# Fetching gamma's row as seven small transfers instead of one, in an RMSNorm and SiLU kernel on one core

## The chip, the cores and the metric

The kernel runs on one core of a Trainium2 chip. The metric is the device time of one execution in microseconds (us), median of three runs. In this document a "load" brings a block of `x` from HBM into on-chip memory and a "store" takes a finished block back. TensorE, VectorE and ScalarE appear in the profile as PE, DVE and ACT; SP and ACT issue the transfers, and their issuing queues appear as SPq and ACTq. The 16 DMA engines of the core move the bytes for both queues. In the tables of DMA queues q10 carries what ACT issues and q1 what SP issues.

## The reference

```python
def reference(x, gamma, eps):          # x: 8 x 1024 x 2048, gamma: 2048, all float32
    rms = np.sqrt(np.mean(x ** 2, axis=-1, keepdims=True) + eps)
    out = gamma * x / rms
    return (out * (1 / (1 + np.exp(-out)))).astype(np.float32)
```

Each of the 8192 rows of 2048 numbers is divided by its root mean square, multiplied by gamma, and put through SiLU. The input is 67.1 MB and so is the output.

## The kernel before

The rows are cut into 16 blocks of 512 rows. A block is one tile `xt` of 128 partitions; each partition holds 4 rows (`J = 4`), so that a load or a store of a block is one transfer of 4 MB in which every partition has one contiguous piece of 32 KB. Six such tiles exist (`BUFS = 6`). The work is done in place: a block is loaded (line 54, issued on ACT's queue), its sums of squares are taken (two or one of its rows by ScalarE, line 65, the others by VectorE, line 73), the root is taken on ScalarE (line 82) and inverted on VectorE (line 87), VectorE multiplies each row by its reciprocal root and by gamma (line 92), ScalarE applies SiLU to the block in two halves (line 98), and SP issues the store (line 102). The last block goes a little differently (lines 153 to 160): it is multiplied by gamma first, and its SiLU takes the reciprocal root as a scale (line 158).

The order of each engine's work is written out by hand. What matters for the change is the head, lines 106 to 119, in the order of the program:

- load 0 is issued on ACT's queue (line 106); VectorE fills the tile `ones` (line 107); ScalarE runs one tiny activation (line 109).
- SP fetches gamma's row, 8 KB, into partition 0 of the tile `g` (line 110), and then issues a small store of `ones` to 16 pieces of 512 bytes in the output's first block (line 111), which store 0 later overwrites.
- TensorE spreads gamma over the 128 partitions: four chunks of 512 columns, each a multiplication of a column of ones with the chunk of the row in partition 0, into `junk_v` in PSUM (line 114). A float32 chunk shows as two matmuls in the profile.
- load 1 is issued on ACT's queue (line 115).
- VectorE copies the whole of `junk_v` back over `g` (line 116), and ScalarE copies one element of `junk_v` (line 117). ScalarE's copy waits for VectorE's.
- Only behind that copy, on ACT's queue, come loads 2 to 5 (lines 118 and 119).

Then the squares of block 0 begin. Inside the main loop, load `b + 3` is issued on ACT's queue after the first row of squares of block `b + 1` (lines 65 to 69). For the first three blocks (`SOON = 3`) the multiplication of block `b` comes ahead of the squares of block `b + 1`; later it comes behind them.

The framework gives each transfer one of eight completion semaphores in turn, in the order of the program, and the queue that issues a transfer first waits until the transfer that had the same semaphore before has landed. In program order the transfers before the change are load 0, gamma, the store of `ones`, loads 1 to 5 (the first eight), then store 0, store 1, store 2, load 6 and so on, 34 in all.

Of the kernel before, what the change touches and what calls it, by code (L numbers as in the profile page):

```python
# [1 line left out]

# [4 lines left out]

ACT = mybir.ActivationFunctionType
ALU = mybir.AluOpType


@with_exitstack
def kernel(
    ctx: ExitStack,
    tc: tile.TileContext,
    x: bass.AP,
    gamma: bass.AP,
    eps: bass.AP,
    out: bass.AP,
):  # L20

    nc = tc.nc
    P = nc.NUM_PARTITIONS
    f32 = mybir.dt.float32
    x2 = x.flatten_outer_dims()
    o2 = out.flatten_outer_dims()  # L30
    n, d = x2.shape
    J = 4
    BUFS = 6
    nblk = n // (P * J)
    xb = x2.rearrange("(b p j) d -> b p (j d)", p=P, j=J)
    ob = o2.rearrange("(b p j) d -> b p (j d)", p=P, j=J)

    singles = ctx.enter_context(tc.tile_pool(name="singles", bufs=1))
    pool = ctx.enter_context(tc.tile_pool(name="pool", bufs=BUFS))
    small = ctx.enter_context(tc.tile_pool(name="small", bufs=2))  # L40
    psum = ctx.enter_context(tc.tile_pool(name="psum", bufs=1, space=bass.MemoryType.PSUM))

    Q = 4
    w = d // Q
    g = singles.tile([P, d], f32)
    eps_t = singles.tile([P, 1], f32)
    ones = singles.tile([P, P], f32)
    junk_a = psum.tile([P, d], f32, name="junk_a")
    junk_v = psum.tile([P, d], f32, name="junk_v")
    blocks, sss, rmss, rstds = {}, {}, {}, {}  # L50

    def load(b):
        xt = pool.tile([P, J * d], f32, name="xt")
        nc.scalar.dma_start(out=xt, in_=xb[b])  # L54
        blocks[b] = xt

    def row(b, j):
        return blocks[b][:, j * d:(j + 1) * d]

    def squares_scalar(b, loads=()):  # L60


        sss[b] = small.tile([P, J], f32, name="ss")
        for j in range(share(b)):
            nc.scalar.activation(out=junk_a, in_=row(b, j), func=ACT.Square,  # L65
                                 accum_out=sss[b][:, j:j + 1])
            if j == 0:
                for s in loads:
                    load(s)

    def squares_vector(b):
        for j in range(share(b), J):
            nc.vector.tensor_tensor_reduce(  # L73
                out=junk_v, in0=row(b, j), in1=row(b, j), scale=1.0, scalar=0.0,
                op0=ALU.mult, op1=ALU.add, accum_out=sss[b][:, j:j + 1])

    def share(b):
        return 1 if 4 <= b <= 12 and b % 2 == 0 else 2

    def root(b):  # L80
        rms = small.tile([P, J], f32, name="rms")
        nc.scalar.activation(out=rms, in_=sss.pop(b), func=ACT.Sqrt, scale=1.0 / d, bias=eps_t)  # L82
        rmss[b] = rms

    def invert(b):
        rstd = small.tile([P, J], f32, name="rstd")
        nc.vector.reciprocal(out=rstd, in_=rmss.pop(b))  # L87
        rstds[b] = rstd

    def multiply(b):  # L90
        for j in range(J):
            nc.vector.scalar_tensor_tensor(out=row(b, j), in0=row(b, j), scalar=rstds[b][:, j:j + 1],  # L92
                                           in1=g, op0=ALU.mult, op1=ALU.mult)

    def silu(b):
        for h in range(0, J, 2):
            cols = slice(h * d, (h + 2) * d)
            nc.scalar.activation(out=blocks[b][:, cols], in_=blocks[b][:, cols], func=ACT.Silu)  # L98
        store(b)

    def store(b):
        nc.sync.dma_start(out=ob[b], in_=blocks[b])

    with tc.manual_schedule():

        load(0)
        nc.vector.memset(ones, 1.0)  # L107
        nc.vector.memset(eps_t, float(eps))
        nc.scalar.activation(out=junk_a[:, 0:1], in_=ones[:, 0:1], func=ACT.Square)  # L109
        nc.sync.dma_start(out=g[0:1, :], in_=bass.AP(tensor=gamma.tensor, offset=gamma.offset, ap=[[d, 1], [1, d]]))  # L110
        nc.sync.dma_start(out=ob[0][::P // 16, 0:P], in_=ones[::P // 16, :])
        for c in range(Q):
            cols = slice(c * w, (c + 1) * w)
            nc.tensor.matmul(junk_v[:, cols], ones[0:1, :], g[0:1, cols], start=True, stop=True)  # L114
        load(1)
        nc.vector.tensor_copy(out=g, in_=junk_v)  # L116
        nc.scalar.copy(out=junk_a[:, 0:1], in_=junk_v[:, d - 1:d])  # L117
        for b in range(2, BUFS):
            load(b)

        last = nblk - 1
        SOON = 3
        squares_scalar(0)
        squares_vector(0)
        root(0)
        invert(0)
        for b in range(last):
            loads = [b + 3] if BUFS <= b + 3 < nblk else []  # L130
            if b < SOON:
                multiply(b)
                squares_scalar(b + 1, loads)
                silu(b)
                squares_vector(b + 1)
                root(b + 1)
            elif b < last - 1:
                squares_scalar(b + 1, loads)
                squares_vector(b + 1)
                root(b + 1)  # L140
                multiply(b)
                silu(b)
            else:
                multiply(b)
                squares_scalar(b + 1)
                silu(b)
                squares_vector(b + 1)
                root(b + 1)
            if b + 1 < last:
                invert(b + 1)  # L150


        for j in range(J):
            if j == J // 2:
                invert(last)
            nc.vector.tensor_mul(out=row(last, j), in0=row(last, j), in1=g)  # L156
        for j in range(J):
            nc.scalar.activation(out=row(last, j), in_=row(last, j), func=ACT.Silu,  # L158
                                 scale=rstds[last][:, j:j + 1])
        store(last)  # L160


# [1 line left out]
_INS = ['x', 'gamma', 'eps']  # L164
_OUTS = [((8, 1024, 2048), 'float32')]

_NUMBERS = {'eps': 9.999999747378752e-06}


# [26 lines left out]
```

## Time and profile before

| what | value |
|---|---|
| median of 3 runs | 316.97 us (316.83 to 317.03) |
| the profiled execution's own time | 316.86 us |
| its span, first to last instruction | 315.1 us |
| VectorE busy | 235.4 us, 75% of the span |
| ScalarE busy | 213.9 us, 68% |
| TensorE matmuls | 7.2 us, 2%, eight matmuls |
| transfers of 4 MB | 16 loads on ACT's queue, 16 stores on SP's queue |
| bytes moved | 134.25 MB, mean 426 GB/s over the span |

The span is shorter than the execution's time by 1.8 us, which lie outside the first and last instruction. The page of the profile cuts the span into 40 equal slices and gives, for each, the busy share of each engine in tenths, the mean busy share of the 16 DMA engines and the rate. Its chain of work is followed back from the last instruction and tells what released what. The waits give, for each engine and line, how long the engine stood and what ended that. A packet, in the tables of DMA queues, is one contiguous piece moved by one DMA engine, or the small write of 4 bytes with which that engine reports that its part of a transfer is done.

### The profile page before, as it was taken

What the parts mean: (1) busy time and instruction counts of PE and PEld (TensorE: products, weight loads), DVE (VectorE), ACT (ScalarE), POOL (GpSimd) and SP (SyncE); (2) the same over time, 40 slices, a digit from 0 to 9 for tenths busy, and PEclk for the clock granted to TensorE, in tenths of its full rate; (3) what the DMA queues carried; (4) which work ended last, traced back from release to release, by engine and by line L of the source; (5) the groups of instructions that cost most, each with busy time, mean ns of one, the idle gap of its engine ahead of it and who ended that gap; (6) DMA issues with size and microseconds to landing.
All of it is one profiled execution on the core that took longest, in us unless ns stands there. A gap on an engine that the chain in (4) does not pass through costs nothing.

```text
span 315.1 us, 440 instructions
## 1 busy us (share of the span) xinstructions
PE 7.2 (2%) x8; PEld 2.5 (1%) x8; DVE 235.4 (75%) x157; ACT 213.9 (68%) x137; POOL 0.2 (0%) x4
## 2 busy tenths in 40 slices
PE   6200000000000000000000000000000000000000
PEld 2000000000000000000000000000000000000000
DVE  0679697979995795957959489593995939999600
ACT  1169998972799268782687727876278768779910
POOL 0000000000000000000000000000000000000000
DMA  8999999999999999999999999999999999999996
GB/s 331 408 458 412 395 458 404 458 412 453 416 454 416 446 416 449 416 449 416 449 420 449 416 449 420 449 416 449 424 441 428 437 433 433 433 433 433 433 433 300
DMA packets 4644, 134.25 MB, mean 426 GB/s; under 512 B 529, under 2 KB 545, under 8 KB 545
## 3 DMA queue, kind: packets, MB, share of 16 engines
q10 hardware_dynamic: 2304, 67.11, 49.7%
q1 hardware_dynamic: 2338, 67.13, 49.4%
q14 instruction: 2, 0.02, 0.0%
HBM read 67.12 MB, written 67.12 MB: 426 GB/s over the span
## 4 chain that ended last, share of the span: by engine, by line
DMA 68%; DVE 14%; ACT 11%; issue 1%; ACTq 1%; DVEq 0%
DMA xt<-in_x_dram 68%; DVE xt L92 9%; DVE junk_v L73 5%; ACT xt L98 4%; ACT junk_a L65 3%; ACT xt L158 2%; ACT L82 1%; ACTq L191 1%; ACT L158 0%; ACT L98 0%; ACT rms L82 0%; DVE ss L73 0%; DVE rstd L87 0%; ACTq L54 0%; ACT L109 0%
## 5 line engine op out<-in xcount | busy, mean ns | idle before, releaser
L92 DVE SCALAR_TENSOR_TENSOR xt<-xt,rstd,g 128x2048 f32<-128x2048 f32 x60 | 137.0, 2346 | 0.1
L98 ACT ACTIVATE xt<-xt 128x4096 f32<-128x4096 f32 x30 | 108.3, 3615 | 27.1 <-DVE xt L92 27.1
L73 DVE CUSTOM_DVE_ANT_0 junk_v<-xt 128x2048 f32<-128x2048 f32 x37 | 85.1, 2299 | 42.4 <-DMA xt<-in_x_dram 41.7
L65 ACT ACTIVATE junk_a<-xt 128x2048 f32<-128x2048 f32 x27 | 50.6, 1876 | 16.1 <-DMA xt<-in_x_dram 14.0
L82 ACT ACT_TABLE_LOAD x15 | 19.2, 1283 | 26.6 <-DVE ss L73 26.5
L98 ACT ACT_TABLE_LOAD x14 | 18.0, 1283 | 0.2
L116 DVE COPY g<-junk_v 128x2048 f32<-128x2048 f32 x1 | 2.3, 2292 | 9.1 <-PE junk_v L114 9.1
L87 DVE RECIPROCAL rstd<-rms 128x4 f32<-128x4 f32 x16 | 2.8, 173 | 8.4 <-ACT rms L82 8.4
L156 DVE TENSOR_TENSOR xt<-xt,g 128x2048 f32<-128x2048 f32 x4 | 9.0, 2280 | 0.0
L82 ACT ACTIVATE rms<-ss,eps_t 128x4 f32<-128x4 f32 x16 | 4.8, 297 | 5.7 <-DVE ss L73 5.5
L158 ACT ACTIVATE xt<-xt,rstd 128x2048 f32<-128x2048 f32 x4 | 7.7, 1991 | 0.0
L114 PE MATMUL junk_v<-g,ones 1*128 1x512 f32 x8 | 7.2, 1072 | 2.9 <-DMA g<-in_gamma_dram 2.9
L117 ACT COPY junk_a<-junk_v 128x1 f32<-128x1 f32 x1 | 0.1, 144 | 9.9 <-DVE g L116 9.9
L73 DVE DVE_READ_ACCUMULATOR2_ANT ss<- 128x1 f32 x37 | 5.2, 140 | 0.0
L65 ACT ACTIVATION_READ_ACCUMULATOR junk_a<-xt 128x1 f32 x27 | 5.0, 186 | 0.0
L114 PEld LDWEIGHTS junk_v<-g,ones 1*128 1x128 f32 x8 | 2.5, 327 | 6.0 <-issue 6.0
L109 ACT ACT_TABLE_LOAD x1 | 1.3, 1283 | 1.1 <-PEq L177 1.1
L158 ACT ACT_TABLE_LOAD x1 | 1.3, 1283 | 0.0
L107 DVE MEMSET ones<- 128x128 f32 x1 | 0.2, 165 | 0.8 <-PEq L177 0.8
L109 ACT ACTIVATE junk_a<-ones 128x1 f32<-128x1 f32 x1 | 0.2, 174 | 0.0
L177 POOL MEMSET const-bfloat16-1.0<- 128x1 bf16 x1 | 0.1, 102 | 0.0
L177 POOL MEMSET const-uint8-127<- 128x1 uint8 x1 | 0.1, 102 | 0.0
(3 smaller groups left out, 0.3 us busy)
## 6 DMA issues: line engine op xcount, KB each, us to landing
xt<-in_x_dram ACTq DMA_DIRECT2D x16, 4096.0 KB, 38.7
out_dram<-xt SPq DMA_DIRECT2D x16, 4096.0 KB, 32.1
g<-in_gamma_dram SPq DMA_DIRECT2D x1, 8.0 KB
out_dram<-ones SPq DMA_DIRECT2D x1, 8.0 KB, 7.1
```

Source lines behind the costliest of these rows:

```text
L65: nc.scalar.activation(out=junk_a, in_=row(b, j), func=ACT.Square, accum_out=sss[b][:, j:j + 1])
L73: nc.vector.tensor_tensor_reduce(out=junk_v, in0=row(b, j), in1=row(b, j), scale=1.0, scalar=0.0, op0=ALU.mult, op1=ALU.add, accum_out=sss ...
L82: nc.scalar.activation(out=rms, in_=sss.pop(b), func=ACT.Sqrt, scale=1.0 / d, bias=eps_t)
L87: nc.vector.reciprocal(out=rstd, in_=rmss.pop(b))
L92: nc.vector.scalar_tensor_tensor(out=row(b, j), in0=row(b, j), scalar=rstds[b][:, j:j + 1], in1=g, op0=ALU.mult, op1=ALU.mult)
L98: nc.scalar.activation(out=blocks[b][:, cols], in_=blocks[b][:, cols], func=ACT.Silu)
L109: nc.scalar.activation(out=junk_a[:, 0:1], in_=ones[:, 0:1], func=ACT.Square)
L114: nc.tensor.matmul(junk_v[:, cols], ones[0:1, :], g[0:1, cols], start=True, stop=True)
L116: nc.vector.tensor_copy(out=g, in_=junk_v)
L156: nc.vector.tensor_mul(out=row(last, j), in0=row(last, j), in1=g)
L158: nc.scalar.activation(out=row(last, j), in_=row(last, j), func=ACT.Silu, scale=rstds[last][:, j:j + 1])
L191: with _tile.TileContext(nc) as tc:
```

## The change

Gamma's row is still fetched by SP from the same place into the same partition, but in seven transfers: six of 256 numbers (1 KB) and a last one of 512 numbers (2 KB). Pieces 0 and 1 make up the first chunk of 512 columns that TensorE multiplies, pieces 2 and 3 the second, 4 and 5 the third, and piece 6 is the whole of the fourth. Nothing else is changed, so there are 40 transfers in place of 34.

```diff
         nc.scalar.activation(out=junk_a[:, 0:1], in_=ones[:, 0:1], func=ACT.Square)
-        nc.sync.dma_start(out=g[0:1, :], in_=bass.AP(tensor=gamma.tensor, offset=gamma.offset, ap=[[d, 1], [1, d]]))
+        piece, pieces = d // 8, 7
+        for k in range(pieces):
+            at = k * piece
+            size = piece if k < pieces - 1 else d - at
+            nc.sync.dma_start(out=g[0:1, at:at + size],
+                              in_=bass.AP(tensor=gamma.tensor, offset=gamma.offset + at, ap=[[d, 1], [1, size]]))
         nc.sync.dma_start(out=ob[0][::P // 16, 0:P], in_=ones[::P // 16, :])
```

## The prediction

> **What bounds the kernel now.** I read the 40 slices first, then the busy time by stretches, then the issues and waits, then the timeline of the head, and last the packet records of the trace. The page:
>
> ```profile
> DMA  8999999999999999999999999999999999999996
> GB/s 331 408 458 412 395 458 404 458 412 453 416 454 416 446 416 449 416 449 416 449 420 449 416 449 420 449 416 449 424 441 428 437 433 433 433 433 433 433 433 300
> ...
> q10 hardware_dynamic: 2304, 67.11, 49.7%
> q1 hardware_dynamic: 2338, 67.13, 49.4%
> ```
>
> The DMA engines are at 9 tenths or more in every slice but the first and last. Busy time in stretches cut at landings (each engine's busy us, granted clock, DMA share, GB/s):
>
> ```profile
> 1.20:13.10 11.90, 7.16 (x8) 2.50 (x8) 2.29 (x1) 1.54 (x3) 0.00 (x0) 1.00 0.97 398
> 13.10:22.80 9.70, 0.00 (x0) 0.00 (x0) 7.42 (x7) 5.58 (x6) 0.00 (x0) 1.00 1.00 432
> ...
> 59.90:279.00 219.10, 0.00 (x0) 0.00 (x0) 175.92 (x118) 149.98 (x93) 0.00 (x0) 1.00 1.00 433
> 279.00:304.50 25.50, 0.00 (x0) 0.00 (x0) 17.21 (x11) 21.56 (x13) 0.00 (x0) 1.00 1.01 434
> ```
>
> From 13 us to 304 us the DMA share is 1.00. The packet records say the same: a 32 KB packet takes 1.213 us, each engine moves 256 of them (32 blocks, 8 each), 310.5 us, and the span is 315.1. The kernel is bound by the service of its DMA engines. So an edit costs time only if DMA engines stand idle for it; shorter waits of DVE or ACT gain nothing. The chain of waits names DVE and ACT for a quarter of the span, but only because it runs through the instructions that issue loads.
>
> What the change touches is the head:
>
> ```profile
> 0.73 0.34 SPq L110 DMA_DIRECT2D g<-in_gamma_dram  x1
> ...
> 1.13 0.54 SPq L111 DMA_DIRECT2D out_dram<-ones  x1
> ...
> 2.88 7.16 PE L114 MATMUL junk_v<-g,ones 1*128 1x512 f32 x8 [2.88 <-DMA g<-in_gamma_dram]
> ...
> 10.07 2.29 DVE L116 COPY g<-junk_v 128x2048 f32<-128x2048 f32 x1 [9.08 <-PE junk_v L114]
> 12.46 0.14 ACT L117 COPY junk_a<-junk_v 128x1 f32<-128x1 f32 x1 [9.86 <-DVE g L116]
> 12.48 1.80 ACTq L54 DMA_DIRECT2D xt<-in_x_dram  x4
> ```
>
> The reader is to see one chain: gamma lands, eight matmuls, DVE's copy, ACT's copy, and only then loads 2 to 5. Loads 0 and 1 cover it: load 1's last packets end at 21.8 to 22.5 us, depending on the engine. Load 2, issued at 12.48, is early.
>
> **The change part by part.** *Seven issues for one.* SP needs 0.40 us from one small issue to the next (0.73 to 1.13), so piece 6 is issued 6 x 0.40 = 2.4 us later, at 3.1. If that were all, gamma would be complete at 2.74 + 2.4 = 5.1 us and nothing would follow.
>
> *Each piece's place in the line.* Before, q1 has 2338 packets: 2304 of the 16 stores, 32 of the store of `ones` (16 of data, 16 completions), which leaves 2 for gamma: it runs on a single DMA engine, one data packet (0.307 us) and one completion. It got through at 2.13 and 2.43 us, just ahead of that engine's first packet of load 0 (2.44); its semaphore rose at 2.74. The later pieces meet load 0. What a small SP transfer then meets is shown by the next row:
>
> ```profile
> out_dram<-ones SPq DMA_DIRECT2D x1, 8.0 KB, 7.1
> ```
>
> It takes 7.1 us to land, although its packets take 0.027 and 0.009 us. In the packet records 15 engines give it this order: three 32 KB packets of load 0, the data at 6.0 to 6.7, one more 32 KB packet, the completion at 7.2 to 8.0. Gamma's engine gives two load packets, data at 4.91, one load packet, completion at 6.15. So a DMA engine with both queues waiting takes one packet from each in turn, and each small one costs a turn of 1.21 us. Seven pieces are 14 packets in one line on one engine (taking it that each piece, like the whole row, runs there).
>
> Piece 0 passes as gamma did. Piece 1 is ready about 0.4 us later, when that engine has taken up load 0. I place it where the store of `ones` stood on this engine, behind two load packets: 4.7 us. From piece 1's data to piece 6's completion there are 11 more turns; one falls on load 0's own 4-byte completion. That is 10 x 1.213 + 0.4 for the small packets, so the last completion is at 17.2 and is seen 0.3 us later, as gamma's was (2.44 to 2.74): 17.5 us. With one load packet ahead instead of two it is 16.3, with three, as on the other engines, 18.7.
>
> A rule speaks against this. The Trainium skill, page "DMA: Bandwidth & Descriptors", section "Queues, rings and completion order", says that an engine changes between queues only after it has drained a whole packet, typically 9 to 17 descriptors. By that rule the 14 small ones could go in one or two turns and the sum would be no loss. The order of the `ones` store, with a load packet between its data and its completion, contradicts it here.
>
> *What follows.* Matmuls of the first three chunks run between the pieces. Behind piece 6 there are two of the eight matmuls: 0.14 to start, 0.87 (the spacing of their starts) + 1.06, then DVE's 2.29 and the 0.15 us that lay around it, and ACT's copy and issue 0.12 later (12.36 to 12.48). Load 2 is issued 4.6 us after piece 6 lands, at 22.1.
>
> *The gap.* How long until an idle DMA engine moves data is shown by load 0 alone: issued at 0.73, and each engine's second packet starts between 3.59 and 4.30. One packet earlier, its first counts as begun 2.37 to 3.08, that is 1.64 to 2.35 us after issue. So load 2 effectively begins at 23.7 to 24.4, where the last engine was free at 22.5: a gap of 1.2 to 1.9 us in a resource that is busy to the end. I take the middle, 1.6. With pieces complete at 16.3 the gap is 0 to 0.7, at 18.7 it is 2.4 to 3.1. The bounds from both sides: nothing, if the pieces got through as fast as the issues allow; 3.1 from the slowest row.
>
> *What is hidden.* The extra packets themselves are 0.1 us on one engine, lost in the gap. The store of `ones` becomes ninth in program order and waits for load 0's landing, 13.1 us (before, store 0 had that wait: SP stood 11.4 us on `DMA xt` there). Behind it on SP is only store 0, issued at 35.35; with 7.1 us it has landed by 21, so nothing. Load 1, tenth, waits for piece 0: issued near 2.8, not at 1.20, while load 0 keeps the engines until 12.1. Loads 2 to 5 and stores 0 and 1 inherit waits for pieces 1 to 6, met long before.
>
> ACT and DVE start on block 0 later. ACT's squares move from 14.4 to 24.0, the multiplication ends near 39, and store 0 moves from 35.4 to about 42.7. The loads queued by then last, alone, until 24.1 + 4 x 9.7 = 63 us, so the engines have work. Afterwards a block costs DVE some 14 us against 19.4 us of DMA for load plus store, so DVE and ACT catch up. At the end store 15 is issued at 300.7 while store 14 lands at 304.5: 3.8 us of cover. It grows, since loads that run alone for longer finish earlier and leave more stores in line. If this cover were gone, ACT's and DVE's end (279 to 300.7) would show instead.
>
> *The sum* against the profiled execution: 316.86 + 1.6 = 318.5 us. That execution is 0.11 below the median of the runs, so I forecast a median of 318.6, which is 0.5% slower. A measurement of this kernel can tell about 0.2%, 0.63 us, from no change.
>
> **The rivals.**
>
> *The pieces do not wait turn by turn, and it is not slower.* The place is gamma's engine between 2.4 and 17 us. For it: gamma's own data and completion went back to back. Then piece 6 lands soon after its issue at 3.1, by 10.2 even with the 7.1 us of the whole `ones` store; load 2 is issued by 14.8 and nothing is lost: 317.0. The point from which it decides: piece 6 landed before about 15.6, because 15.6 + 4.6 + 2.35 = 22.5. Against it: the order of the `ones` store.
>
> *All chunks wait for the last piece.* If the waits are not kept by columns, eight matmuls follow piece 6, 5.1 us more: load 2 at 27.2, a gap of 6.7, 323.7. Against it: ACT's SiLU of a half block starts at 268.93 while DVE still multiplies rows of the same block (268.81 to 273.42), so waits do go by columns.
>
> *The pieces are issued one after the other's landing.* If writes to one tile were put in order, each would need its issue, two or three turns and a completion, about 5 us: six of them bring piece 6 to some 33 us, load 2 to 37, and a gap of 16: 333. Against it: the same waits by columns; pieces don't overlap.
>
> **How the numbers follow.** The turn-by-turn case has 0.72: inside it 0.06 lies within 0.2% (one load packet ahead and a quick restart), the rest is slower. No waiting by turns has 0.18: 0.15 within 0.2%, 0.03 faster by luck of how the engines line up. All chunks waiting has 0.06 and pieces in series 0.04. So slower 0.76, within 0.2% 0.21, faster 0.03. The range takes in the first two cases, from 316.9 (no gap) to 320.3 (gap 3.1, 0.2 for the runs' spread), and leaves out the last two.
>
> **What would show it.** PE's last two matmuls starting between 16.4 and 19 us after a wait on gamma, in place of eight together at 2.88; the four load issues near 22 instead of 12.48; a dip in the DMA share between 22 and 25; block 0's first store near 43; after that the same 433 GB/s to the end. I would be wrong if the four issues came before about 20 us (then no gap), or if a second dip came later, which would mean that the compute chain does not catch up.

## The result, and the profile after

The changed kernel takes 318.9 us, median of five runs (318.79 to 319.37), beside 316.99 us (316.83 to 317.16) for the kernel before in five runs. The ratio is 1.0065, with a 95% interval of 1.005 to 1.008: slower by 0.65%. The forecast was 318.6, range 316.9 to 320.3. The profiled execution took 318.87 us, its span is 317.1 us; before, these were 316.86 and 315.1.

The page's rate in the 40 slices and SP's queue:

```profile
GB/s 327 418 377 401 438 393 426 451 409 455 405 460 414 446 426 438 442 418 446 409 463 401 459 418 442 434 426 446 413 451 413 459 409 451 422 438 442 418 446 285
...
q1 hardware_dynamic: 2350, 67.13, 49.1%
```

The third slice (15.9 to 23.8 us) fell from 458 to 377 GB/s, and there are 12 packets more, one of data and one completion for each of the six added transfers. The head of the changed kernel, from the timeline (start, duration, engine, line, what; in brackets the idle time before and what ended it; line 114 is now gamma's pieces, 116 the store of `ones`, 119 the matmuls, 121 and 122 the two copies):

```profile
0.73 2.20 SPq L114 DMA_DIRECT2D g<-in_gamma_dram  x7
...
2.00 0.33 ACTq L54 DMA_DIRECT2D xt<-in_x_dram  x1
...
6.42 2.04 PE L119 MATMUL junk_v<-g,ones 1*128 1x512 f32 x2 [6.42 <-DMA g<-in_gamma_dram]
...
11.36 2.04 PE L119 MATMUL junk_v<-g,ones 1*128 1x512 f32 x2 [2.90 <-DMA g<-in_gamma_dram]
13.51 0.54 SPq L116 DMA_DIRECT2D out_dram<-ones  x1
...
15.09 2.04 PE L119 MATMUL junk_v<-g,ones 1*128 1x512 f32 x2 [1.69 <-DMA g<-in_gamma_dram]
...
17.51 2.07 PE L119 MATMUL junk_v<-g,ones 1*128 1x512 f32 x2 [0.38 <-DMA g<-in_gamma_dram]
19.62 2.29 DVE L121 COPY g<-junk_v 128x2048 f32<-128x2048 f32 x1 [18.62 <-PE junk_v L119]
22.00 0.14 ACT L122 COPY junk_a<-junk_v 128x1 f32<-128x1 f32 x1 [19.39 <-DVE g L121]
22.03 1.86 ACTq L54 DMA_DIRECT2D xt<-in_x_dram  x4
```

All seven pieces are issued within 2.2 us, but TensorE gets them two at a time until 17.5 us, and loads 2 to 5 are issued at 22.03 us in place of 12.48. What that does to the DMA engines is read from the stretches around it (the last two numbers are the DMA share and GB/s; a share over 1 is a stretch in which packets begin that end outside it). The first is the stretch that had a share of 1.00 and 432 GB/s before:

```profile
13.10:22.80 9.70, 4.42 (x5) 0.99 (x4) 2.91 (x2) 0.14 (x1) 0.00 (x0) 1.00 0.88 380
...
20.00:21.00 1.00, 0.00 (x0) 0.00 (x0) 1.00 (x1) 0.00 (x0) 0.00 (x0) 1.00 1.06 459
21.00:22.00 1.00, 0.00 (x0) 0.00 (x0) 0.91 (x1) 0.00 (x0) 0.00 (x0) 1.00 0.23 98
22.00:23.00 1.00, 0.00 (x0) 0.00 (x0) 0.82 (x1) 0.14 (x1) 0.00 (x0) 1.00 0.00 0
23.00:24.00 1.00, 0.00 (x0) 0.00 (x0) 1.00 (x1) 0.00 (x1) 0.00 (x0) 1.00 1.87 524
24.00:25.00 1.00, 0.00 (x0) 0.00 (x0) 0.97 (x3) 1.00 (x1) 0.00 (x0) 1.00 0.23 98
```

No packet of data begins between 22 and 23 us (328 GB/s in that stretch before). From there on nothing is lost again: the same stretch that ran at 433 GB/s before runs at 433 now, and the end is as full:

```profile
59.90:279.00 219.10, 0.00 (x0) 0.00 (x0) 186.59 (x124) 161.73 (x103) 0.00 (x0) 1.00 1.00 433
279.00:304.50 25.50, 0.00 (x0) 0.00 (x0) 13.35 (x9) 17.72 (x11) 0.00 (x0) 1.00 1.00 432
304.50:314.20 9.70, 0.00 (x0) 0.00 (x0) 0.00 (x0) 0.00 (x0) 0.00 (x0) 1.00 1.00 432
```

### The profile page after: what moved, and what is told of

Its sections match the earlier page's. It is cut to its first block, busy times and chain, and to the rows that moved or that the text cites. A ratio compares the mean times of both kernels' runs of the same rounds, so it can differ in the third digit from the quotient of the medians.

```text
span 317.1 us, 452 instructions
## 1 busy us (share of the span) xinstructions
PE 8.2 (3%) x8; PEld 2.0 (1%) x8; DVE 235.0 (74%) x157; ACT 213.5 (67%) x137; POOL 0.2 (0%) x4
## 4 chain that ended last, share of the span: by engine, by line
DMA 50%; DVE 24%; ACT 13%; issue 4%; ACTq 1%; PE 1%; SPq 1%; DVEq 0%
DMA out_dram<-xt 24%; DMA xt<-in_x_dram 21%; DVE xt L92 14%; DVE junk_v L73 9%; ACT xt L98 5%; DMA g<-in_gamma_dram 5%; ACT junk_a L65 3%; ACT L82 2%; ACT xt L163 2%; DVE g L121 1%; PE junk_v L119 1%; ACTq L196 1%; ACT rms L82 1%; SPq L114 1%; ACTq L54 1%
## 5 line engine op out<-in xcount | busy, mean ns | idle before, releaser
L119 PE MATMUL junk_v<-g,ones 1*128 1x512 f32 x8 | 8.2, 1125 | 11.4 <-DMA g<-in_gamma_dram 11.4
```

## The experiments

The theory is the prediction's: small packets of one queue take turns with the other queue's 32 KB packets, so that gamma is complete at 17.5 us; loads 2 to 5 wait for it; the DMA engines run dry for about 2 us and never make that up. Two rivals: "count" (each of the six extra transfers costs 0.3 us of its own, whatever waits for it) and "compute" (block 0's work starts some 8 us late, and that reaches the end).

### Take the loads out of the wait

```diff
-        load(1)
+        for b in range(1, BUFS):
+            load(b)
         nc.vector.tensor_copy(out=g, in_=junk_v)
         nc.scalar.copy(out=junk_a[:, 0:1], in_=junk_v[:, d - 1:d])
-        for b in range(2, BUFS):
-            load(b)
```

> Seven pieces as in the changed kernel, but loads 2 to 5 are issued right behind load 1, ahead of ScalarE's copy that waits for gamma. Gamma is as late as before this edit (last piece near 17.5 us) and block 0's work too (first store near 42.7). Theory (the DMA engines stand idle because load 2 is issued at 22.0): no gap, 317.0. Rival 'compute' (block 0's work, 7 us late, pushes the end): 318.9. Rival 'count' (each of the six extra transfers costs 0.3 us by itself): 318.9.

Measured: 316.93 us, ratio 0.9999 (0.999 to 1.0007). From its timeline (lines 122 and 123 are here the copies):

```profile
6.43 6.73 ACTq L54 DMA_DIRECT2D xt<-in_x_dram  x4
...
17.65 2.07 PE L119 MATMUL junk_v<-g,ones 1*128 1x512 f32 x2 [0.39 <-DMA g<-in_gamma_dram]
...
28.98 2.35 DVE L92 SCALAR_TENSOR_TENSOR xt<-xt,rstd,g 128x2048 f32<-128x2048 f32 x1
```

Gamma is as late as in the changed kernel, and block 0's multiplication begins at 28.98 us (20.27 before the change, 29.89 in the changed kernel). Only the four load issues are early, and the whole loss is gone. Both rivals fall: 40 transfers and a compute chain 8.7 us late cost nothing that a measurement of this kernel can tell.

### Hold the loads back without any extra transfer

The kernel before, with spare activations on ScalarE ahead of loads 2 to 5 (work that the kernel doesn't need; the output is unchanged):

```diff
         nc.scalar.copy(out=junk_a[:, 0:1], in_=junk_v[:, d - 1:d])
+        for _ in range(5):
+            nc.scalar.activation(out=junk_a, in_=g, func=ACT.Square)
         for b in range(2, BUFS):
             load(b)
```

> One transfer for gamma, as in the kernel before, and five spare activations of 1.88 us on ScalarE (squares of g into junk_a, not used) between its one-element copy and loads 2 to 5, so that these are issued near 22.0 in place of 12.5. 34 transfers. Theory (late issue of load 2): a gap as in the changed kernel, 318.9. Rival 'count': no extra transfers, 317.0. Rival 'compute': ScalarE's part of block 0 is 9.5 us late, 318.9 too; the run with the loads moved ahead tells these two apart.

Measured: 317.52 us, ratio 1.0027 (1.0013 to 1.004), with runs from 317.06 to 319.32. The size was missed, by a step that I had not seen:

```profile
12.35 9.53 ACT L119 ACTIVATE junk_a<-g 128x2048 f32<-128x2048 f32 x5
...
20.00 1.80 ACTq L54 DMA_DIRECT2D xt<-in_x_dram  x4
```

The activations end at 21.9, but ACT's queue issues the loads at 20.0, when the fifth activation begins. By the prediction's reckoning a gap opens from about 20 us, and in this trace there is none: on each engine load 2's packets follow load 1's. Why the runs spread so far is open. In the profiled execution, one of the longer ones (318.05), 15 of the 16 engines finish at 313.0 to 313.8 us, as before the change, and one at 314.66. With six activations (the same edit, `range(6)`):

> As the run with five spare activations, but six: there the queue issued loads 2 to 5 at 20.0 us, while the fifth activation was still running, which is just at the point from which a gap opens. With six the issue comes near 21.9, as in the changed kernel, with 34 transfers. Theory: 318.8. Rival 'count': 317.0 to 317.5, as with five.

Measured: 319.38 us, ratio 1.0069 (1.0055 to 1.0083). Loads 2 to 5 were issued at 22.27. So 34 transfers, gamma complete before 3 us, and the loss of the changed kernel is back through the late loads alone.

### The same number of transfers, waited for or not

The kernel before, with six spare transfers of 1 KB of gamma into a scratch tile that nothing reads, behind gamma's own:

```diff
         nc.sync.dma_start(out=g[0:1, :], in_=bass.AP(tensor=gamma.tensor, offset=gamma.offset, ap=[[d, 1], [1, d]]))
+        for k in range(6):
+            at = k * 256
+            nc.sync.dma_start(out=spare[0:1, at:at + 256],
+                              in_=bass.AP(tensor=gamma.tensor, offset=gamma.offset + at, ap=[[d, 1], [1, 256]]))
```

> Gamma in one transfer, and behind it six spare transfers of 1 KB of gamma into a scratch tile that nothing reads: 40 transfers, with the same semaphores in turn and the same packets on the same DMA engine. Theory: gamma lands at about 2 to 2.8 us, loads 2 to 5 are issued near 12.5, no gap, 317.0. Rival 'count': 318.9.

Measured: 316.97 us, ratio 0.9995 (0.9986 to 1.0003). The loads were issued at 12.43. With the loop moved ahead of gamma's transfer:

> The same six spare transfers of 1 KB, but ahead of gamma's one transfer. Theory: gamma's two packets are last in a line of 14, one turn each, landing near 17.7; all eight matmuls come after it (7.2 us), loads 2 to 5 are issued near 27.3, the engines stand idle from 22.5, and the time is 318.9 + 5.3 = 324.2. Rival 'count': 318.9, as the same number of transfers. A line without turns: 317.0.

Measured: 324.48 us, ratio 1.0232 (1.0219 to 1.0245). Its head:

```profile
2.67 0.31 SPq L115 DMA_DIRECT2D g<-in_gamma_dram  x1
...
18.09 7.16 PE L119 MATMUL junk_v<-g,ones 1*128 1x512 f32 x8 [18.09 <-DMA g<-in_gamma_dram]
...
27.70 1.89 ACTq L55 DMA_DIRECT2D xt<-in_x_dram  x4
```

One transfer of 8 KB, issued at 2.67 us, is there at 18.0, because six small ones stand ahead of it in the same line. The same 40 transfers cost nothing or 2.3%, depending only on whether gamma is last.

### More pieces and fewer

In the changed kernel, `pieces` is 4 (with `d // 4` each), 6 or 8.

> Four pieces of 2 KB, one for each chunk: 37 transfers. Theory, counting 1.21 us for each turn of the line: last piece lands near 11.2, load 2 is issued near 15.8, ahead of the 20 us from which a gap opens: 317.0. Rival 'count' (0.32 us for each transfer above 34): 318.0.

Measured: 317.35 us, ratio 1.0012 (1.0003 to 1.002). Its last two matmuls start at 11.71 and the loads are issued at 16.22: no gap in the head, as expected. The 0.3 us that remain are at the edge of what can be told; no run looks for their place.

> Eight pieces of 1 KB: 41 transfers. Theory: the eighth piece needs two turns more, lands near 19.9, load 2 is issued near 24.5, 2.45 us later than with seven, all of it a gap: 321.3. (The eighth piece shares load 0's semaphore and is issued only after load 0 has landed, near 13.5, while its place in the line comes at 18.3, so that adds nothing.) Rival 'count': 319.2.

Measured: 321.53 us, ratio 1.0143 (1.0129 to 1.0156); the loads were issued at 24.83. Two turns more, 2.6 us more.

> Six pieces, five of 1 KB and a last one of 3 KB, which holds half of the third chunk and all of the fourth, so that four matmuls follow it: 39 transfers. Theory: last piece lands near 15.1, load 2 is issued near 21.4, 0.6 us earlier than with seven, 318.3. Rival 'count': 318.6.

Measured: 320.17 us, ratio 1.01 (1.0086 to 1.0114). This expectation was wrong, and in an instructive way:

```profile
11.88 5.45 PE L119 MATMUL junk_v<-g,ones 1*128 1x512 f32 x6 [2.90 <-DMA g<-in_gamma_dram]
13.03 0.34 ACTq L54 DMA_DIRECT2D xt<-in_x_dram  x1
...
19.79 1.88 ACTq L54 DMA_DIRECT2D xt<-in_x_dram  x4
```

The loads 2 to 5 are early enough. It is load 1 that is late: with six pieces and the store of `ones` between them it falls eight transfers behind load 0, gets load 0's semaphore, and ACT's queue holds it until load 0 has landed. The engines run dry there instead: from 12 to 13 us their share is 0.02, from 13 to 14 it is 0.00. The packet records add something on the line: once load 0 had passed, pieces 4 and 5 went through in 0.2 us (data at 12.62 and 12.67, completions at 12.67 and 12.79), where two pieces took 4.9 us beside load 0. With nothing in the other queue, there are no turns to wait for. I tried to give load 1 another semaphore by moving its line:

```diff
+        load(1)
         nc.sync.dma_start(out=ob[0][::P // 16, 0:P], in_=ones[::P // 16, :])
...
-        load(1)
```

> Six pieces once more, with load 1 ahead of the store of ones in program order. In the first run with six, load 1 was the eighth transfer after load 0, got its semaphore and was issued only at 13.0, after load 0 had landed. Now the store of ones has that place. Theory: load 1 is issued early, the last piece (3 KB) lands near 15.1, four matmuls follow, load 2 is issued near 21.3, 0.7 us earlier than with seven pieces: 318.2. If the 3 us of the first run with six came from something else than load 1's late issue: 320.2 again.

Measured: 319.92 us, ratio 1.0093 (1.008 to 1.0107). The edit did not do what it was for: in this trace the store of `ones` still has the seventh of the other semaphores and load 1 still that of load 0, issued at 13.14. So the semaphores do not always follow the order of the text, though they do in both kernels compared here; what decides their order, no run shows. What six pieces cost with an early load 1 was therefore not measured.

### What sets the length of a turn

> Seven pieces, but load 0 is issued as four transfers of 1 MB, one for each row of a partition, so that its packets are 8 KB, and gamma's transfers come first in program order (which changes only who shares a semaphore). Theory: a turn in the line lasts as long as one packet of the other queue, so it costs 0.30 us instead of 1.21 while load 0 runs: the 12 packets behind piece 0 need about 4 us, gamma is complete near 8, load 2 is issued near 12.5, no gap: 317.0. If a turn costs 1.2 us whatever the other queue's packets are, gamma completes near 17.5: 318.9. Rival 'count' (43 transfers): 319.9.

Measured: 320.23 us, ratio 1.0106 (1.009 to 1.0121).

> Load 0 as four transfers of 1 MB with packets of 8 KB, this time first in program order, so that no part of load 0 shares a semaphore with a piece of gamma before it. Pieces 4, 5 and 6 share those of the first three quarters of load 0 and are issued after these have landed (about 5, 7.5 and 10 us). Theory: a turn costs one 8 KB packet, 0.30 us; pieces 1 to 3 are through by about 6.5 (at 1.21 us a turn they would need until 11), the last lands near 12.5, load 2 is issued near 17, no gap in any place: 317.0. If a turn costs 1.2 us whatever the packets are: last piece near 17.5, 318.9.

Measured: 319.89 us, ratio 1.009 (1.0076 to 1.0104). Both totals say nothing on turns, and for the reason just met: the second quarter of load 0 had the semaphore of the first, and was issued only at 5.5 us, when the first had landed; the third and fourth had those of pieces 1 and 2 (in the second trace too, in spite of the order of the text). So the engines ran dry at the start, and from 5 us on the pieces passed with nothing beside them. Only piece 1 met packets of 8 KB: its data and its completion lie 0.35 us apart (4.42 and 4.76 in the first trace, 4.10 and 4.45 in the second), where 32 KB packets make it 1.25. From the second run's stretches:

```profile
5.00:8.00 3.00, 3.00 (x4) 1.39 (x5) 0.00 (x0) 1.16 (x1) 0.00 (x0) 1.00 0.50 135
```

The last run changes the packets without adding a transfer: in blocks 0 and 1 a partition takes rows `j * 128 + p` in place of four neighbouring ones, in the load and in the store.

```diff
+    def part(flat, whole, b):
+        if b > 1:
+            return whole[b]
+        return flat[b * P * J:(b + 1) * P * J].rearrange("(j p) d -> p j d", p=P, j=J)
...
-        nc.scalar.dma_start(out=xt, in_=xb[b])
+        nc.scalar.dma_start(out=view(xt, b), in_=part(x2, xb, b))
```

> The changed kernel with seven pieces and the same 40 transfers, but blocks 0 and 1 take their rows in another order (row j of a partition is row 128 j + p of the block, for the load and for the store), so that each 4 MB load and store of these two blocks is moved in packets of 8 KB in place of 32 KB. No transfer is added, so no semaphore is shared otherwise than in the changed kernel. Theory (a turn in the line costs one packet of the other queue): 0.30 to 0.35 us a turn, the last piece lands near 9, load 2 is issued near 13.5, no gap: 317.0 to 317.4. If a turn costs 1.2 us whatever the packets of the other queue are: last piece near 17.5, load 2 near 22, 318.9.

Measured: 317.87 us, ratio 1.0029 (1.0018 to 1.0041). From its timeline and its stretches:

```profile
5.14 7.42 PE L127 MATMUL junk_v<-g,ones 1*128 1x512 f32 x8 [5.14 <-DMA g<-in_gamma_dram]
...
15.01 1.79 ACTq L62 DMA_DIRECT2D xt<-in_x_dram  x4
```

```profile
18.00:21.00 3.00, 0.00 (x0) 0.00 (x0) 1.91 (x2) 2.95 (x5) 0.00 (x0) 1.00 1.03 429
21.00:22.00 1.00, 0.00 (x0) 0.00 (x0) 0.00 (x0) 1.00 (x1) 0.00 (x0) 1.00 1.00 418
22.00:23.00 1.00, 0.00 (x0) 0.00 (x0) 0.38 (x2) 0.54 (x2) 0.00 (x0) 1.00 1.56 664
```

The same seven pieces are through by 8.7 us in place of 17.1: in the packet records a turn is 0.33 us (data of piece 3 at 6.26, its completion at 6.61, data of piece 4 at 6.92), where it was 1.23 us beside 32 KB packets. There is no gap; TensorE runs its eight matmuls in 7.42 us, almost without a pause (7.16 in the kernel before). The time is nevertheless 0.85 us above the kernel before, not within 0.4 as expected. The packets of 8 KB took 0.309 to 0.318 us in the records, against 1.213 / 4 = 0.303; an engine has 128 of them in the two blocks, so 0.7 to 1.9 us in all, and 0.9 by the mean of the records without the slow first packets. Load 1's last packets end at 22.4 to 22.8, about 0.4 later than before. That fits, and is not tested further.

### One line through the runs

| run | load 2 issued, us | time, us |
|---|---|---|
| spare transfers behind gamma | 12.43 | 316.97 |
| before | 12.48 | 316.99 |
| four pieces | 16.22 | 317.35 |
| held by five activations | 20.00 | 317.52 |
| seven pieces | 22.03 | 318.9 |
| held by six activations | 22.27 | 319.38 |
| eight pieces | 24.83 | 321.53 |
| spare transfers ahead of gamma | 27.70 | 324.48 |

The issue is read from the profiled execution, the time is the median of all. The table has the runs that differ in nothing else that bears on the DMA engines: those in which they ran dry at another place, the one with 8 KB packets, and the one whose loads do not wait for gamma (issued from 6.43 us, 316.93) are left out. Below 20 us the issue of load 2 hardly matters. From 22.03 to 27.70, 5.67 us later, the time grows by 5.6: one for one. The line through these meets 317.0 at 20.1 us. Number of transfers and number of pieces do not order this table; the issue of load 2 does. No kernel here beats the one before by more than can be told.

## Why the prediction was right

**What bounds the kernel.** Right: the time moved with idle DMA engines. A compute chain 8.7 us late was free.

**The line of 14 packets.** Right, almost to the packet. In the records piece 1's data passes at 4.69 us (4.7 forecast, two load packets ahead), the others every 2.47 us, with the one short turn at load 0's own completion (12.09 and 12.14), and piece 6's completion at 17.11 (17.2). Its semaphore rose at 17.47 (17.5). The place of piece 1 in the line was a choice among three; it held here, and in the records of the other seven runs with several small transfers beside 32 KB packets the second of them passes at 4.81 to 5.22.

**The rule that spoke against it.** The Trainium skill, page "DMA: Bandwidth & Descriptors", section "Queues, rings and completion order", has an engine drain a packet of typically 9 to 17 descriptors before it changes queues. Here it changed after each single piece, of 32 KB (1.23 us a turn) or 8 KB (0.33 us), and the measurement decides. (The records show contiguous pieces and completions, not descriptors as such.) The rival that the pieces don't wait turn by turn is excluded by this.

**From gamma to load 2.** Right: 22.03 us against 22.1. The waits go by columns: the first two matmuls start at 6.42, on two pieces of seven. That excludes the rivals with all chunks waiting and with pieces in series; SP issued the pieces 0.28 to 0.40 us apart (0.40 forecast).

**The gap.** The mechanism held, the size was a little low: 1.6 forecast, 2.0 in the profiled execution (318.87 - 316.86), 1.9 between the medians. The engines' second packets of load 2 start at 24.80 to 25.44, so that the first count as begun 1.56 to 2.20 us after the issue, as load 0 had shown (1.64 to 2.35). The other end of the gap was set too late: the prediction counted every engine's gap from 22.5, when the last engine was free. In the packet records of the changed kernel the engines end load 1 at 21.8 to 22.8, on average at 22.1, and load 2 counts as begun at 23.9 on average, so that an engine stood 1.8 us in the mean. The ends moved by as much, from 313.3 to 315.1 on average, so nothing was made up. The kernel ends with its last engine, and that one finished 2.2 later: before the change at 313.71, now at 315.92, while the other 15 finish at 314.80 to 315.30. Why one is later than the rest is open.

**What was called hidden.** It was. Load 1 came at 2.00 (2.8 forecast), the store of `ones` at 13.51, behind load 0, and landed 6.7 us later; store 0 was issued at 42.70 (42.7 forecast). The cover at the end grew: store 15 was issued at 296.8 us and store 14 landed at 306.6, which is 9.8 us of cover in place of 3.8. One thing said ahead of the prediction was too simple, that semaphores go by the order of the program; it spoilt three runs, pieces_6b and the two with load 0 in quarters.

## What to carry to other kernels

A small transfer that meets large ones of the other queue on a DMA engine waited here a turn for each of its packets, and a turn lasted one packet of the large transfer (1.23 us at 32 KB, 0.33 us at 8 KB): so count the packets in that line, not the bytes, and keep whatever is waited for first in it. In a kernel that is bound by DMA, ask of every wait only whether a load is queued behind it and how long the loads already issued last; the same lateness cost 0 or 2 us here according to that alone. When transfers are added, look in the trace for which earlier transfer each one shares its semaphore with.

## What the runs showed of the hardware that was not expected

- ACT's queue issued transfers 1.9 us before the activation ahead of them had ended (20.0 against 21.9 us with five activations, 22.27 against 24.14 with six): these transfers, which depend on no result of it, did not wait for its end.
- The kernel went on in another rhythm at the same rate. In the changed kernel the median time from issue to landing fell for loads and rose for stores (38.7 and 32.1 us before):

```profile
xt<-in_x_dram ACTq DMA_DIRECT2D x16, 4096.0 KB, 12.7
out_dram<-xt SPq DMA_DIRECT2D x16, 4096.0 KB, 42.5
```

  The first store starts 7.3 us later, and three times ScalarE, whose queue issues the loads, stood for `DMA out_dram<-xt`, 8.6 us in all. A reading that fits, and that no run tests: the loads run ahead, and later ones wait for a store to free their tile. The DMA share stays 1.00 all the same.
- Packets of 8 KB took 2 to 5% more time for their bytes than packets of 32 KB in the same kernel.
